# A hybrid decoder step on one core: matmul order pinned by hand, or left to the scheduler under the same priorities

## The chip, the core and the metric

The kernel runs on one core of a Trainium2 chip. The core has TensorE (matmul, PE in the profile), VectorE (DVE), ScalarE (ACT), GpSimd (POOL) and the SP queue, which issues all DMAs here. Each engine works through its own list of instructions in order and waits on semaphores where an operand comes from another engine. The metric is the time of one execution on the device in microseconds, the median of the runs.

## The reference, cut to what matters

One inference step of a one-layer decoder for 1024 prompt tokens and 8 x 4 sample tokens, model width 1024. All is in 32-bit floats.

```
h = RMSNorm(x);  z = h @ w_in            # 7944 columns, split among mixers and gates
ya = gated DeltaNet(z_a)                  # 4 heads of 128: conv, SiLU, chunked delta rule
yb = RWKV-7(z_b)                          # 8 heads of 64: shift, LoRA decay, delta state update
yc = RG-LRU(z_c)                          # conv, gates, diagonal scan
x = x + (sum_b sigmoid(z_gate_b) * (y_b @ w_branch[b])) @ w_out
x = x + relu(RMSNorm(x) @ w_up)^2 @ w_down
y = RMSNorm(x)
```

The two delta rules are recurrences over tokens. Both are written in chunks: inside a chunk a triangular matrix of products of keys is inverted, and between chunks a state is handed on, so each chunk's output waits for the state of the one before.

## The kernel before

**Projections.** Every large product is computed as three matmuls of a 128x128 weight with a 128x352 slice of the tokens (high by high, low halves by high), on PSUM tiles named g, whose rotation has two buffers. `weights` loads a weight tile (wraw), ScalarE rounds it to its high half (whi, L342), and VectorE or, in the recurrence, GpSimd subtracts to get the low half (wlo, L343). `gemm_steps` is a generator: one step is three matmuls, and a projection of 128 output channels is 24 steps of 72 matmuls in all. ScalarE copies the result out (z).

**The recurrence.** After the start (norm, the RG-LRU branch, and half of the projections of branches A and B) comes a stage of 18 units. A unit is one segment of 128 tokens (one of every nine is the 32 sample tokens) of two RWKV head pairs (`rwkv_seg`) and two DeltaNet heads (`gdn_seg`), with one joint inversion of their triangular blocks. The steps of a unit that the change and the trace speak of:

- Gram matmuls: rr<-AR,BK (L1092), masked by VectorE into GM (L1095). AR and BK are products that VectorE and GpSimd form (L1070 to L1083); the two halves of the first BK product run on GpSimd, those of the second on VectorE (L1080 to L1082).
- `inv16_load`: GM and LA are written to DRAM and read back as rows of 16x16 blocks, i16m (L842 to L846).
- `inv16_solve`: some 24 VectorE operations on 48 rows invert these blocks (L858 to L886); the result i16z goes to DRAM and comes back as i16u (L894, L897).
- `tri`: it is spread (ixt, L903), transposed (ix, L924) and completed to 64x64 and 128x128 inverses (inv, TT) in alternating matmuls (rr<-ix,GM and others) and copies.
- The links: sr<-N,AR (with the old state N), tm (L1181), sr<-tm,inv, UV (L1185, L1186), sr<-UV,BT and sr<-UV,GM, then the new N (L1217, L1218). There are two links to a unit. DeltaNet's one link is sg<-St,kq, gtm, sg<-gtm,TT, gu, sg<-gu,kv, St.
- Reciprocal square roots, `rsqrt` (L641 to L652): an integer guess and three Newton steps on 128x2 or 128x4 numbers, 13 operations on GpSimd, three times a unit: tile nwyg for the keys' norm, nwyo and nwyr for the two output norms.

**What sets the order.** A scheduler builds each engine's list. It takes the ready instruction of highest priority, by its own estimate of when operands are ready; priority is program order unless `high_priority` raises it, and `keep_in_program_order` fixes an instruction in the list where the program has it. Program order comes from `PLAN` (L1474), a table of 19 places: at each, some steps of the new unit ("n..") or of the old one ("o..") are issued, and then `fill.go(2)` issues two steps (six matmuls) of the projections still to do: in units 0 to 8 the other half of branches A and B, then the merge gates. While the stage runs (`T.on`), `Ordered._pin` fixes every TensorE instruction at its place, the old unit's steps and the inversion get high priority on the other engines, and projections that are left when the units are done follow in `fill.rest()`. All TensorE work passes through `Ordered`, so the profile of the kernel before gives one line for all matmuls (L259) and one for all transposes (L262); they are told apart by tile names.

**Behind the stage** come the merge of the branches, the output projection and the feed-forward part, nearly all projections.

Of the kernel before, what the change touches and what calls it, by code (L numbers as in the profile page):

```python
# [10 lines left out]
I32 = mybir.dt.int32  # L11
# [237 lines left out]
class Ordered:  # L249


    def __init__(self, tc, eng):
        self.tc, self.eng, self.on = tc, eng, False

    def _pin(self, r):
        return self.tc.keep_in_program_order(r) if self.on else r

    def matmul(self, *a, **kw):
        return self._pin(self.eng.matmul(*a, **kw))  # L259

    def transpose(self, *a, **kw):
        return self._pin(self.eng.transpose(*a, **kw))  # L262


# [30 lines left out]
class K:  # L295
    def __init__(self, tc, ctx, ap):
        self.tc, self.nc, self.ap = tc, tc.nc, ap
        self.ctx = ctx
        self.V, self.A, self.P, self.T, self.S = (tc.nc.vector, tc.nc.scalar, tc.nc.gpsimd, Ordered(tc, tc.nc.tensor), tc.nc.sync)
        self.n = 0  # L300
        self.lo_eng = tc.nc.vector
# [127 lines left out]
def build(tc, ap):  # L429
    nc = tc.nc  # L430
    with ExitStack() as ctx:
# [209 lines left out]
        def rsqrt(x, shape, tag):  # L641

            yi = k.tile(mp, shape, "nwy" + tag, 2, I32)
            t = k.tile(mp, shape, "nwt" + tag, 1)
            P.tensor_scalar(out=yi, in0=x.bitcast(I32), scalar1=-0.5, scalar2=1597463007.0, op0=ALU.mult, op1=ALU.add)
            y = yi.bitcast(F32)
            for _ in range(3):
                P.tensor_tensor(out=t, in0=y, in1=y, op=ALU.mult)
                P.tensor_tensor(out=t, in0=t, in1=x, op=ALU.mult)
                P.tensor_scalar(out=t, in0=t, scalar1=-0.5, scalar2=1.5, op0=ALU.mult, op1=ALU.add)  # L650
                P.tensor_tensor(out=y, in0=t, in1=y, op=ALU.mult)
            return y  # L652
# [328 lines left out]
        def prio():  # L981

            return nullcontext() if T.on else tc.high_priority()
# [16 lines left out]
        def rwkv_seg(R, seg, J):  # L1000

            s2, lora = R["s2"], R["lora"]
            if True:
# [76 lines left out]
                for src, j, e in ((kk, 0, P), (zk, 1, V)):  # L1080
# [380 lines left out]
        T.on = True  # L1461
# [16 lines left out]
        for i in range(19):  # L1478
            after_ = None
            for what, f in PLAN:  # L1480
                for w_ in what.split():
# [5 lines left out]
                    elif w_ in ("load", "solve"):  # L1487
                        if new:
                            with tc.high_priority():
                                (inv16_load if w_ == "load" else inv16_solve)(new["J"])  # L1490
                    else:
                        u = new if w_[0] == "n" else old
                        if u:
                            with tc.high_priority() if w_[0] == "o" else nullcontext():
                                next(u[w_[1]], None)
# [5 lines left out]
        T.on = False  # L1501
# [183 lines left out]
```

## Time and profile before

| | |
|---|---|
| median of 3 runs | 2503.41 us (2502.68 to 2505.58) |
| the profiled execution | 2511.07 us, its span 2509.3 us |
| TensorE busy | 2183.4 us, 87% of the span |
| VectorE, ScalarE, GpSimd busy | 1178.8, 816.8, 512.2 us |
| mean granted TensorE clock | 0.925 |
| the stage of 18 units | about 380 to 1430 us |

The page's second part cuts the span into 40 slices of 62.7 us, each digit the busy share in tenths. A wait view says which engine stood still for whose result; a timeline shows each instruction with its start, its duration and, in brackets, the idle time of its engine before it and what ended that. A matmul of the small kind stands as two records in the trace, so counts there are twice those of the program's order. Busy times of a matmul overlap its neighbours'; the distance between two starts is what one costs.

### The profile page before, as it was taken

To read this page: it belongs to the slowest core of one execution; us is meant where nothing else is said; L and a number is where in the kernel's file an instruction comes from. 1 tells how busy PE (TensorE), PEld (TensorE's weight loads), DVE (VectorE), ACT (ScalarE), POOL (GpSimd) and SP (SyncE) were. 2 spreads that over 40 slices of the span, in tenths; PEclk is the share of its full clock that TensorE was granted. 3 is DMA by queue.
4 is the path that set the end of the run, shared out by engine and by line. 5 is a ranking of instruction groups with operands and counts; after the bars stand their busy time and mean duration, and the time that the engine had idled before them with its cause. 6 is when DMAs were issued, how large, how long until landed. Compare 5 with 4: busy or idle time off the path is not lost. (4 is left out here: it accounts for less than half of the span.)

```text
span 2509.3 us, 42716 instructions
## 1 busy us (share of the span) xinstructions
PE 2183.4 (87%) x16939; PEld 2042.7 (81%) x16939; DVE 1178.8 (47%) x2490; ACT 816.8 (33%) x1915; POOL 512.2 (20%) x1213
## 2 busy tenths in 40 slices
PE   8999987776667677777777899999999999999997
PEld 7998986666556565666656799999999999999997
DVE  7453353555555544455445205747433433333336
ACT  5564342333333332243333222225221221221224
POOL 2013233333324223233343220013000000000003
PEclk9999996888887887888888899999999999999999
DMA  4114331222222222222221335433111111111114
GB/s 132 67 57 135 101 100 57 77 66 55 56 60 69 62 66 77 57 68 64 62 55 50 106 129 193 151 120 109 43 46 48 47 47 43 51 43 47 47 44 148
DMA packets 171713, 191.59 MB, mean 76 GB/s; under 512 B 60853, under 2 KB 114293, under 8 KB 171513
## 3 DMA queue, kind: packets, MB, share of 16 engines
q1 hardware_dynamic: 171512, 188.87, 24.6%
q8 instruction: 133, 2.18, 0.4%
q14 instruction: 68, 0.55, 0.1%
HBM read 140.68 MB, written 48.13 MB: 75 GB/s over the span
## 5 line engine op out<-in xcount | busy, mean ns | idle before, releaser
L259 PE MATMUL g<-hhi,whi 128*128 128x352 f32 x2664 | 904.5, 346 | 15.3 <-DVE z L419 14.0
L259 PE MATMUL g<-hhi,wlo 128*128 128x352 f32 x2568 | 848.5, 330 | 0.9 <-POOL wlo L343 0.9
L259 PE MATMUL g<-hlo,whi 128*128 128x352 f32 x2472 | 819.3, 331 | 4.6 <-DVE hlo L561 3.4
L259 PEld LDWEIGHTS g<-hhi,whi 128*128 128x128 f32 x2664 | 516.4, 195 | 34.6 <-DVE z L419 16.1
L259 PEld LDWEIGHTS g<-hhi,wlo 128*128 128x128 f32 x2568 | 501.1, 195 | 2.2 <-POOL wlo L343 1.4
L259 PEld LDWEIGHTS g<-hlo,whi 128*128 128x128 f32 x2472 | 485.4, 196 | 9.3 <-DVE hlo L561 4.5
L342 ACT CAST whi<-wraw 128x512 fp32r<-128x512 f32 x326 | 200.9, 619 | 558.2 <-PE g L259 545.8
L259 PE MATMUL g<-ahi,wlo 128*128 128x352 f32 x768 | 248.4, 323 | 0.0
L259 PE MATMUL g<-ahi,whi 128*128 128x352 f32 x768 | 248.3, 323 | 0.0
L259 PE MATMUL g<-alo,whi 128*128 128x352 f32 x768 | 248.1, 323 | 0.0
L1586 POOL TENSOR_TENSOR acc<-acc,sq 128x352 f32<-128x352 f32 x36 | 37.2, 1033 | 913.3 <-ACT sq L1585 912.7
L343 DVE TENSOR_TENSOR wlo<-wraw,whi 128x512 fp32r<-128x512 f32 x216 | 151.6, 703 | 146.8 <-ACT whi L342 142.8
L343 POOL TENSOR_TENSOR wlo<-wraw,whi 128x512 fp32r<-128x512 f32 x110 | 147.4, 1343 | 338.9 <-ACT whi L342 322.6
L1647 DVE TENSOR_TENSOR x<-g,x 128x352 f32<-128x352 f32 x192 | 100.4, 524 | 201.1 <-PE g L259 201.1
L259 PE MATMUL rr<-ix,GM 32*32 32x32 f32 x816 | 19.0, 224 | 171.0 <-DVE ix L924 171.0
L259 PEld LDWEIGHTS rr<-ix,GM 32*32 32x32 f32 x816 | 14.7, 134 | 178.2 <-DVE ix L924 129.3
L259 PEld LDWEIGHTS g<-ahi,wlo 128*128 128x128 f32 x768 | 144.8, 189 | 0.1
L259 PEld LDWEIGHTS g<-ahi,whi 128*128 128x128 f32 x768 | 144.6, 188 | 0.2
L259 PEld LDWEIGHTS g<-alo,whi 128*128 128x128 f32 x768 | 144.6, 188 | 0.1
L1636 DVE TENSOR_TENSOR rl<-rl,g 128x352 f32<-128x352 f32 x96 | 49.8, 519 | 133.5 <-ACT rl L1635 133.5
L1635 ACT ACTIVATE rl<-g 128x352 f32<-128x352 f32 x96 | 44.4, 463 | 138.5 <-PE g L259 138.5
L1638 DVE TENSOR_TENSOR alo<-rl,ahi 128x352 fp32r<-128x352 f32 x96 | 50.4, 525 | 47.5 <-ACT ahi L1637 47.5
(354 smaller groups left out, 2920.6 us busy)
## 6 DMA issues: line engine op xcount, KB each, us to landing
wraw<-win SPq DMA_DIRECT2D x126, 256.0 KB, 2.7
wraw<-wdn SPq DMA_DIRECT2D x80, 256.0 KB, 2.6
wraw<-wup SPq DMA_DIRECT2D x64, 256.0 KB, 2.6
scr_t<-z SPq DMA_DIRECT2D x24, 528.0 KB, 3.2
tgl<-scr_t SPq DMA_DIRECT2D x24, 528.0 KB, 4.1
scr_za<-z SPq DMA_DIRECT2D x16, 528.0 KB, 3.0
wraw<-wout SPq DMA_DIRECT2D x32, 256.0 KB, 2.6
scr_zb<-z SPq DMA_DIRECT2D x12, 528.0 KB, 2.7
```

Source lines behind the costliest of these rows:

```text
L259: return self._pin(self.eng.matmul(*a, **kw))
L342: self.A.copy(hi, r3)
L343: self.lo_eng.tensor_tensor(out=lo, in0=r3, in1=hi.bitcast(F32), op=ALU.subtract)
L1586: (V if last else P).tensor_tensor(out=acc[g], in0=acc[g], in1=sq, op=ALU.add)
L1635: A.activation(out=rl, in_=ps, func=AF.Relu)
L1636: V.tensor_tensor(out=rl, in0=rl, in1=ps, op=ALU.mult)
L1638: V.tensor_tensor(out=b[:, gl(g)], in0=rl, in1=a[:, gl(g)].bitcast(F32), op=ALU.subtract)
L1647: V.tensor_tensor(out=x2[c][:, gl(g)], in0=ps, in1=x2[c][:, gl(g)], op=ALU.add)
```

## The change

TensorE's instructions are no longer pinned: `Ordered` is gone, and a flag `k.busy` takes over its other use (it keeps the extra priority of some elementwise steps off during the stage). The raised priority of the old unit's steps and of the inversion is gone too, so within the stage program order alone is the priority on all engines, apart from the weights' halves and the copies out of PSUM. `rsqrt` moves from GpSimd to VectorE, with two operations of a Newton step merged: 10 operations instead of 13. The first BK product moves from GpSimd to VectorE.

```diff
--- before.py
+++ after.py
@@ -246,22 +246,6 @@
 
 
 
-class Ordered:
-
-
-    def __init__(self, tc, eng):
-        self.tc, self.eng, self.on = tc, eng, False
-
-    def _pin(self, r):
-        return self.tc.keep_in_program_order(r) if self.on else r
-
-    def matmul(self, *a, **kw):
-        return self._pin(self.eng.matmul(*a, **kw))
-
-    def transpose(self, *a, **kw):
-        return self._pin(self.eng.transpose(*a, **kw))
-
-
 def run(gen):
 
     while True:
@@ -296,8 +280,9 @@
     def __init__(self, tc, ctx, ap):
         self.tc, self.nc, self.ap = tc, tc.nc, ap
         self.ctx = ctx
-        self.V, self.A, self.P, self.T, self.S = (tc.nc.vector, tc.nc.scalar, tc.nc.gpsimd, Ordered(tc, tc.nc.tensor), tc.nc.sync)
+        self.V, self.A, self.P, self.T, self.S = (tc.nc.vector, tc.nc.scalar, tc.nc.gpsimd, tc.nc.tensor, tc.nc.sync)
         self.n = 0
+        self.busy = False
         self.lo_eng = tc.nc.vector
 
     def pool(self, name, bufs=1, side=None, psum=False):
@@ -642,13 +627,12 @@
 
             yi = k.tile(mp, shape, "nwy" + tag, 2, I32)
             t = k.tile(mp, shape, "nwt" + tag, 1)
-            P.tensor_scalar(out=yi, in0=x.bitcast(I32), scalar1=-0.5, scalar2=1597463007.0, op0=ALU.mult, op1=ALU.add)
+            V.tensor_scalar(out=yi, in0=x.bitcast(I32), scalar1=-0.5, scalar2=1597463007.0, op0=ALU.mult, op1=ALU.add)
             y = yi.bitcast(F32)
             for _ in range(3):
-                P.tensor_tensor(out=t, in0=y, in1=y, op=ALU.mult)
-                P.tensor_tensor(out=t, in0=t, in1=x, op=ALU.mult)
-                P.tensor_scalar(out=t, in0=t, scalar1=-0.5, scalar2=1.5, op0=ALU.mult, op1=ALU.add)
-                P.tensor_tensor(out=y, in0=t, in1=y, op=ALU.mult)
+                V.tensor_tensor(out=t, in0=y, in1=y, op=ALU.mult)
+                V.scalar_tensor_tensor(out=t, in0=t, scalar=-0.5, in1=x, op0=ALU.mult, op1=ALU.mult)
+                V.scalar_tensor_tensor(out=y, in0=t, scalar=1.5, in1=y, op0=ALU.add, op1=ALU.mult)
             return y
 
         def store_tail(dst, z, sv, hist):
@@ -980,7 +964,7 @@
 
         def prio():
 
-            return nullcontext() if T.on else tc.high_priority()
+            return nullcontext() if k.busy else tc.high_priority()
 
         def rwkv_gemm(s2):
             lo = k.tile(mp, [128, 2, 3, 128], "lora", 1)
@@ -1077,7 +1061,7 @@
                 for i in range(2):
                     A.activation(out=pr(av, i), in_=pr(av, i), func=AF.Identity, scale=k.p("bka", 2 * s2 + i), bias=k.d("oka", 2 * s2 + i))
                 V.tensor_tensor(out=ch(zk), in0=ch(zk), in1=ch(av), op=ALU.mult)
-                for src, j, e in ((kk, 0, P), (zk, 1, V)):
+                for src, j, e in ((kk, 0, V), (zk, 1, V)):
                     for h in range(2):
                         e.tensor_tensor(out=BK[H[h], 0:nb, j if h == 0 else 1 - j, 0:tl], in0=ch(src)[H[h]], in1=ch(ei)[H[h]], op=ALU.mult)
                 V.tensor_tensor(out=ar(1), in0=ch(zr), in1=ch(eg), op=ALU.mult)
@@ -1458,7 +1442,7 @@
             return r, g
 
         rb, ra = run(rwkv_gemm(0)), run(gdn_gemm(0))
-        T.on = True
+        k.busy = True
         fill = Filler(second_half())
 
         def unit(i):
@@ -1486,19 +1470,16 @@
                         after_ = unit(i + 1) if i < 17 else None
                     elif w_ in ("load", "solve"):
                         if new:
-                            with tc.high_priority():
-                                (inv16_load if w_ == "load" else inv16_solve)(new["J"])
+                            (inv16_load if w_ == "load" else inv16_solve)(new["J"])
                     else:
                         u = new if w_[0] == "n" else old
                         if u:
-                            with tc.high_priority() if w_[0] == "o" else nullcontext():
-                                next(u[w_[1]], None)
+                            next(u[w_[1]], None)
                 fill.go(f)
             if i == 0:
                 fill.go(14)
             new, old = after_, new
         fill.rest()
-        T.on = False
         mp_cm.__exit__(None, None, None)
 
         mg_cm = k.pool("mrg", side="left")
```

What this does to the order, at three places. Line numbers of the changed kernel are 16 to 19 lower.

First, TensorE between DeltaNet's last step and the Gram matmuls of the next unit, in the unit of masks GM_1715; g tiles are projections. Before:

```order
L259 MATMUL sr_11288<-tm_11289,inv_11074 64x64 x4
L259 MATMUL sg_11273<-gu_11270,kv_10541 128x128 x2
L259 MATMUL sg_11273<-gu_11270,LA_10540 128x128 x2
L259 MATMUL rr_11346<-kq_10854 128x256
L259 MATMUL rr_11352<-kq_10854 128x256
L259 MATMUL g_11303<-hhi,whi_10992 128x352
L259 MATMUL g_11303<-hlo,whi_10992 128x352
L259 MATMUL g_11303<-hhi,wlo_10993 128x352
L259 MATMUL g_11303<-hhi,whi_10992 128x352
L259 MATMUL g_11303<-hlo,whi_10992 128x352
L259 MATMUL g_11303<-hhi,wlo_10993 128x352
L259 MATMUL rr_11365<-AR_11083,BK_11084 128x128
```

The same place in the changed kernel:

```order
L1076 MATMUL rr_11248<-AR_10972,BK_10973 128x128
L1145 MATMUL sr_11108<-UV_10756,BT_10675 64x64 x4
L1145 MATMUL sr_11108<-UV_10756,GM_10662 64x64 x4
L1076 MATMUL rr_11249<-AR_10972,BK_10973 128x128
L1076 MATMUL rr_11248<-AR_10972,BK_10973 128x128
L1076 MATMUL rr_11249<-AR_10972,BK_10973 128x128
L1076 MATMUL rr_11248<-AR_10972,BK_10973 128x128
L1076 MATMUL rr_11249<-AR_10972,BK_10973 128x128
L1076 MATMUL rr_11248<-AR_10972,BK_10973 128x128
L1076 MATMUL rr_11249<-AR_10972,BK_10973 128x128
L1085 MATMUL rr_11261<-con,BK_10973 128x128
L1145 MATMUL sr_11174<-N_11151,AR_10371 64x64 x8
```

Six projections stand no longer between DeltaNet's step and the Gram matmuls; the first link's last matmuls (sr<-UV) stand among them, and the second link (sr<-N,AR) behind them, where it stood ahead.

Second, TensorE behind the output transposes of DeltaNet (rr<-con,oa) in that unit. Before:

```order
L262 MATMUL rr_11549<-con,oa_11268 128x128 x2
L259 MATMUL g_11542<-hhi,whi_11481 128x352
L259 MATMUL g_11542<-hlo,whi_11481 128x352
L259 MATMUL g_11542<-hhi,wlo_11482 128x352
L259 MATMUL g_11542<-hhi,whi_11481 128x352
```

Changed:

```order
L1413 MATMUL rr_11429<-con,oa_11154 128x128
L1145 MATMUL sr_11693<-N_11289,AR_10972 64x64 x3
L1413 MATMUL rr_11429<-con,oa_11154 128x128
L1145 MATMUL sr_11693<-N_11289,AR_10972 64x64 x5
L340 MATMUL g_12063<-hhi,whi_12059 128x352
L341 MATMUL g_12063<-hlo,whi_12059 128x352
```

The first matmuls of the next unit's first link (sr<-N,AR) now stand here, ahead of that unit's inverse. Counted in the order, the projections between the matmuls rr<-con,k (L1242) and the next rr<-ix,GM are 18 before and 64 in the changed kernel.

Third, VectorE from the masks to the solve. Before:

```order
L1095 TENSOR_TENSOR GM_10770<-rr_10771,con 128x512
L1095 TENSOR_TENSOR GM_10770<-rr_10772,con 128x512
L1217 TENSOR_TENSOR N_10812<-sr_10695,N_10656 128x128
L1229 TENSOR_REDUCE mv_10816<-k_1685_10613 128x4
L1218 TENSOR_TENSOR N_10812<-N_10812,wc_9915 128x128
L1230 TENSOR_SCALAR mv_10816<-mv_10816 128x4
L1231 TENSOR_TENSOR k_1685_10613<-k_1685_10613,mv_10816 128x256
L1126 TENSOR_TENSOR zv_10233<-rr_10879,zv_10233 128x256
L1233 TENSOR_REDUCE mv_10816<-k_1723_10815 128x4
L1234 TENSOR_SCALAR mv_10816<-mv_10816 128x4
L1236 TENSOR_TENSOR k_1685_10613<-k_1685_10613,nwyr_10823 128x256
L858 COPY i16z_10906<-i16m_10795 48x8
```

Changed, the rows just ahead of the solve (L842 there is L858 before):

```order
L1321 TENSOR_TENSOR ar_11237<-con,gr_10740 128x128
L1217 TENSOR_REDUCE mv_10708<-k_1723_10707 128x4
L1414 SCALAR_TENSOR_TENSOR zg_9570<-rr_10828,d_hang,zg_9570 128x256
L1218 TENSOR_SCALAR mv_10708<-mv_10708 128x4
L630 TENSOR_SCALAR nwyr_10715<-mv_10708 128x4
L633 TENSOR_TENSOR nwtr_10716<-nwyr_10715 128x4
L634 SCALAR_TENSOR_TENSOR nwtr_10716<-nwtr_10716,mv_10708 128x4
L635 SCALAR_TENSOR_TENSOR nwyr_10715<-nwtr_10716,nwyr_10715 128x4
L633 TENSOR_TENSOR nwtr_10716<-nwyr_10715 128x4
L634 SCALAR_TENSOR_TENSOR nwtr_10716<-nwtr_10716,mv_10708 128x4
L842 COPY i16z_10795<-i16m_10687 48x8
L853 COPY i16z_10795<-i16m_10687 48x4x2x2
```

The root of the RWKV output norm (nwyr) ran on GpSimd between the two rows mv and k; now its steps stand in VectorE's list, some ahead of the solve and some between its first steps, and DeltaNet's output product zg stands ahead of it.

## Rows read from the trace of the kernel before

**Rows 1.** The page, parts 1 and 2: busy times, TensorE's slices, its granted clock.
```profile
PE 2183.4 (87%) x16939; PEld 2042.7 (81%) x16939; DVE 1178.8 (47%) x2490; ACT 816.8 (33%) x1915; POOL 512.2 (20%) x1213
PE   8999987776667677777777899999999999999997
PEclk9999996888887887888888899999999999999999
```

**Rows 2.** The waits: engine, line waited for: total us, times, longest.
```profile
PE rr L259 <- DVE ix L924: 171.0, 18, 12.6
DVE k L1236 <- POOL nwyr L651: 55.9, 17, 3.7
DVE gsl L1320 <- POOL nwyg L651: 27.2, 17, 3.8
```

**Rows 3.** Line L924 alone: durations in ns, first and last start.
```profile
L924 DVE STREAM_TRANSPOSE ix<-ixt x18: 311/378/379, 380.3 to 1388.8; 128x192 f32<-128x192 f32 x16, 128x128 f32<-128x128 f32 x2
```

**Rows 4.** Windows: busy us by engine, granted clock, DMA share, GB/s.
```profile
1061.00:1115.00 54.00, 39.38 (x466) 34.33 (x466) 28.14 (x73) 18.94 (x59) 18.21 (x51) 0.88 0.27 74
1430.00:1525.00 95.00, 94.63 (x596) 94.34 (x595) 13.72 (x17) 26.70 (x46) 16.50 (x12) 1.00 0.48 162
1800.00:1900.00 100.00, 100.00 (x625) 100.00 (x624) 39.41 (x72) 22.69 (x44) 0.00 (x0) 1.00 0.15 48
```

**Rows 5.** Timeline of TensorE, one unit: start us, us, operation, [idle before].
```profile
1006.41 0.65 PE L259 MATMUL rr<-ix,GM 32*32 32x32 f32 x32 [8.34 <-DVE ix L924]
1007.96 0.49 PE L259 MATMUL g<-hhi,wlo 128*128 128x352 f32 x1
1008.25 0.49 PE L259 MATMUL g<-hhi,whi 128*128 128x352 f32 x1
1033.61 1.16 PE L259 MATMUL rr<-AR,BK 64*128 64x128 f32 x16
1051.39 0.32 PE L259 MATMUL g<-hhi,wlo 128*128 128x352 f32 x1
1061.12 0.65 PE L259 MATMUL rr<-ix,GM 32*32 32x32 f32 x32 [9.40 <-DVE ix L924]
```

**Rows 6.** A window behind such a wait.
```profile
1008.00:1010.00 2.00, 2.00 (x53) 1.61 (x52) 0.00 (x0) 0.92 (x2) 0.22 (x1) 0.50 0.03 8
```

**Rows 7.** Timeline of VectorE, the same unit.
```profile
1023.44 1.61 DVE L1082 TENSOR_TENSOR BK<-zk,k 64x256 f32<-64x256 f32 x2
1034.80 1.29 DVE L1095 TENSOR_TENSOR GM<-rr,con 128x512 f32<-128x512 f32 x2 [0.63 <-PE rr L259]
1046.33 1.48 DVE L1236 TENSOR_TENSOR k<-k,nwyr 128x256 f32<-128x256 f32 x1 [3.70 <-POOL nwyr L651]
1047.74 0.16 DVE L858 COPY i16z<-i16m 48x8 f32<-48x8 f32 x1
1048.00 0.16 DVE L870 TENSOR_TENSOR i16t<-i16z 48x8 f32<-48x8 f32 x1
1048.20 0.17 DVE L871 TENSOR_TENSOR i16z<-i16z,i16t 48x8 f32<-48x8 f32 x1
1060.29 0.36 DVE L903 TENSOR_TENSOR ixt<-i16u,con 128x192 f32<-128x192 f32 x1 [5.81 <-DMA i16u<-scr_i]
```

**Rows 8.** Timeline of GpSimd, the same unit.
```profile
1042.72 0.19 POOL L645 TENSOR_SCALAR nwyr<-mv 128x4 int32<-128x4 int32 x1 [1.72 <-DVE mv L1234]
1046.25 1.28 POOL L343 TENSOR_TENSOR wlo<-wraw,whi 128x512 fp32r<-128x512 f32 x1
```

**Rows 9.** Timeline of the SP queue, the same unit.
```profile
1039.24 0.33 SPq L846 DMA_DIRECT2D i16m<-scr_i  x1
```

**Rows 10.** Line L846, read back of the Gram matrix: time to landing.
```profile
DMA to landing us min/median/max: 1.9/2.5/3.5
```

**Rows 11.** Lines L1082 and L1236 alone: ns min/median/max.
```profile
L1082 DVE TENSOR_TENSOR BK<-zk,k x36: 216/422/2040, 355.1 to 1352.0; 64x256 f32<-64x256 f32 x32, 64x64 f32<-64x64 f32 x4
...
L1236 DVE TENSOR_TENSOR k<-k,nwyr x18: 281/426/1489, 448.3 to 1420.4; 128x256 f32<-128x256 f32 x16, 128x128 f32<-128x128 f32 x2
```

## The prediction

> **What bounds the kernel now.** I read the page from the top, then the waits of TensorE, then one unit of the recurrence on the timelines. The reader sees first that TensorE is busy 87% of the span, and that the loss has one place: the slices from about 380 to 1430 us stand at 6 to 8 tenths with a granted clock of 0.8, while the slices of the last third stand at 9 and 9 [rows 1]. In that third 625 matmuls fill 100 us, so a projection matmul of 352 columns costs 0.160 us at the full clock [rows 4]. The staged stretch is therefore where a new order can give or take anything. Its beat is one unit of the recurrence; the inverse's transpose (L924) stands once in each of 18 units, from 380.3 to 1388.8 us, which is 1008.5 / 17 = 59.3 us a unit [rows 3]. A quiet unit is 54 us [rows 4].
>
> Among TensorE's waits one rules: 171.0 us in 18 waits for that same transpose [rows 2], 9.5 us a unit. The timeline of a unit shows why [rows 5, 7 to 9]. The unit's Gram matmuls (AR, BK) start at 1033.61, the masks at 1034.80, the matrix is read back from DRAM at 1039.24, the 16x16 solve starts at 1047.74, its result is back at 1060.29, and TensorE, idle since 1051.7, starts on it at 1061.12. So a unit has two parts. Part A runs from one inverse to the next masks, 1006.41 to 1034.80, 28.4 us; part B from the masks to the inverse, 1034.80 to 1061.12, 26.3 us, and for its last 9.4 us TensorE has nothing. After such a wait the granted clock is 0.50, that is 1.2 GHz [rows 6], and the projection matmuls come 0.29 us apart [rows 5].
>
> **The change part by part.** *Tail.* Counted in the order of the two programs, the matmuls on g tiles behind the last unit's second product of its inverse (rr<-ix,GM, L943) are 6684 before and 6448 after: 236 projections are drawn into the staged stretch. They leave a stretch in which TensorE is busy 94.63 of 95 us [rows 4], so they give 236 x 0.160 = 37.8 us there. Inside, their cover is the idle time before the inverse: 13 matmuls a unit, 2.1 us of 9.5. If that cover is gone they cost the same 37.8 us and this term is 0.
>
> *Part A.* From inverse to Gram matmuls the old order has 54 projections and about 135 small matmuls, in nearly every unit (96 in the first); the new one 23 to 43 projections, mostly about 33 (50 in the first), and about 100 small ones. What left is the old unit's second link, and the first link of the next, which now stands before the inverse. That is 21 projections less, 21 x 0.160 = 3.4 us (6.1 us if all ran at 0.29), and some 35 small ones, which I estimate at 2 us (the eight Gram matmuls, two records each and the dearest kind, take 1.16 us [rows 5], 0.145 each; the links' are 64x64 and I count 0.04 to 0.07, which gives 1.4 to 2.5). TensorE's part is thus 4.8 to 8.6 us shorter; I take 5.4. What is late next is VectorE: its last BK product ends at 1025.05 [rows 7], 18.6 us behind the inverse, so A cannot fall under some 20 us while TensorE was the later of the two by 8.6. Into this part VectorE takes over the ten-step root of the keys and the beta product. A dependent small operation follows another by 0.20 us [rows 7], so ten cost 2.0 us; the two beta halves cost 0.42 us each at the median of the same product there [rows 11]. Against that stand VectorE's waits for GpSimd's root, 27.2 us in 17 = 1.6 a unit [rows 2]. Sum: +2.8 - 1.6 = +1.2, which I round up to +1.4. Part A: -5.4 + 1.4 = -4.0 us. Its bounds are 0 and -7.2 (8.6 less 1.4).
>
> *Part B.* The read back is issued 4.4 us behind the masks [rows 7, 9] and lands 2.5 us later [rows 10], at 1041.7. VectorE takes the solve up only at 1047.74: it stands at L1236 for GpSimd's root, from 1042.72 on, 55.9 us in 17 waits = 3.3 us a unit over the kernel [rows 2, 7, 8]. That wait goes. What is late next is VectorE itself: between masks and solve it now has some 28 rows, the whole output root and half of the other among them. At 0.20 us for the small half and 0.3 to 0.45 for the rest that is about 8.5 us, so the solve starts 8.5 us behind the masks and no longer 12.9: -4.4. The rest of the root steps and zg then lie between the solve's own, about eight more at 0.20 = +1.4 (where an operation stands, it is not free). Another +1.5 I allow for the hops of that root through ScalarE to TensorE and back, on which zg now waits in front of the solve. Sum -1.5 us, with -4.4 and +4 (all twenty root steps at 0.20 in the way and nothing gained) as bounds. Behind TensorE's Gram matmuls the new order has 81 to 113 projections instead of 60, so 92 x 0.160 + 80 x 0.055 = 19 us of work; it still reaches the inverse early, and the wait shrinks from 9.5 to about 5 us. That this wait is covered is not a gain of its own: the loop over DRAM sets part B.
>
> *GpSimd and SP.* GpSimd loses 39 root steps and two products a unit; it was on no bound. SP's order keeps the solve's store behind the y stores and one z store, as before, and nothing on it is dearer.
>
> At one place a rule can be weighed. GpSimd's low-half subtraction starts at 1046.25 and takes 1.28 us; VectorE's product with the root starts at 1046.33 and takes 1.48 us [rows 7, 8], where the median of that line's 18 is 0.43 [rows 11]. The Trainium skill, SBUF — State Buffer, section "SBUF: two separate sides", says that the two engines share a port pair under an exclusive lock, and that a VectorE operation with two SBUF inputs waits out a GpSimd one in full. By that rule nearly all root steps can be held so, but 41 fewer GpSimd instructions a unit stand against them; that the trace agrees is seen in these two rows.
>
> **The sum.** Per unit -4.0 - 1.5 = -5.5 us, 18 times -99.0, tail -37.8: -136.8 us. The profiled execution took 2511.07 us (its span of 2509.3 and 1.8 around it), which gives 2374.3; the runs' median, 2503.41, lies 7.7 under that execution, so 2366.6, and I say 2366 us. A difference under 0.2% (5 us) can't be told from no change.
>
> **The rivals.** *The chain links lose their cover, and it is slower.* In the old order six projections, about 1 us, stand behind every link of the recurrence; in the new one the second link's matmuls stand among small ones alone, and TensorE waits for each answer in order, with what is queued behind. For it: TensorE runs in order, and a wait brings the clock to 0.50 [rows 6]. Against it: the old wait of 9.5 us is far larger than these. Eight links uncovered by 1.1 us each are +8.8, less the 4.0 of part A = +4.8 us a unit: 2503.4 + 18 x 4.8 - 37.8 = 2552 us. It decides from the point at which part A of a quiet unit is longer than today's 28.4 us. Chance 0.15.
>
> *The loop over DRAM and VectorE keeps its beat.* What TensorE saves in part A it then waits before the masks; only the tail is left: 2503.4 - 37.8 = 2466 us. For it: VectorE is busy 28.1 of 54 us [rows 4] and gets about 5 more. Against: TensorE was 8.6 us behind VectorE at the Gram matmuls. Chance 0.12.
>
> *VectorE and GpSimd collide.* As in the pair of rows above, each low-half subtraction that meets a root step holds it 1.1 us; three meetings a unit beyond today's are +3.3 us, 18 times 59: 2366 + 59 = 2425 us. Against it: GpSimd is busy 18 of 54 us today and about half of that after. Chance 0.13. This is also what the rule named above would make of the change if GpSimd's remaining work met it.
>
> *It does more.* If A falls to the 21 us that VectorE needs and B by its bound of 4.4, a unit loses 7.2 + 4.4 = 11.6 us: 2503.4 - 208.8 - 37.8 = 2257 us. A middle of this and the forecast, 2310, is likelier than the end. Chance 0.13 for all below 2320.
>
> That the change spreads the projections is not what the order shows: it gathers 64 of them before the inverse and thins them between the links. The argument above does not need them spread.
>
> **How the numbers follow.** The forecast has 0.47, its own range is 2320 to 2430. Low is 2285, between the forecast and the full gain, which leaves about 0.08 below; high is 2500, past the case of the tail alone, and leaves the most of the slower rival, about 0.12. Faster by over 0.2%: the forecast, the collisions, the tail alone and the larger gain, 0.85 less some 0.05 for their far ends, 0.80. Slower 0.15, and 0.05 for within 0.2%.
>
> **What would show it.** The transposes of the inverse 53 to 54 us apart on the mean; TensorE's wait for them near 5 us a unit; Gram matmuls about 24 us behind the inverse in a quiet unit; the solve starting about 8.5 us behind the masks, with no wait for GpSimd's roots; a granted clock over 0.9 in the staged stretch; the bare stretch before the merge shorter by 38 us. I am wrong if new waits of TensorE on sr and sg tiles add up to more than the wait on ix gives back, or if part B grows because the roots stand in the solve's way.

## The result and the profile after

The changed kernel takes 2224.81 us (median of 4, 2220.14 to 2227.51) against 2504.29 (2502.68 to 2505.58): a ratio of 0.888, interval 0.886 to 0.890. It is 280 us faster; 138 had been forecast, and the range ended at 2285. The direction was right, the size was not. Where executions of one kernel differ, ratios leave out those more than 1.5% above its fastest.

First the page of the changed kernel, parts 1 and 2, as in [rows 1].

```profile
PE 2137.2 (96%) x16939; PEld 2003.5 (90%) x16939; DVE 1236.4 (56%) x3066; ACT 817.3 (37%) x1915; POOL 349.8 (16%) x475
PE   8998999999999999999999999999999999999997
PEclk9999999999999999999999999999999999999998
```

The dip of 6 to 8 tenths is gone: TensorE has the same 16939 matmul records and is busy in 96% of a span that is 291 us shorter: 245 us less idle time (326 to 81 us) and 46 us less busy time, at a higher clock. The windows show where the time went: first the stage (from the first to the last inverse) and a stretch behind it in the kernel before, then the same two in the changed one (columns as in [rows 4]). The stretch holds the projections that are left and the beginning of the merge; its end lies equally far from the end of both kernels.

```profile
380.00:1389.00 1009.00, 735.75 (x7870) 622.42 (x7870) 510.37 (x1316) 329.42 (x1007) 338.96 (x941) 0.84 0.23 63
1430.00:1590.00 160.00, 159.63 (x1004) 159.34 (x1003) 53.99 (x87) 38.53 (x62) 16.50 (x12) 1.00 0.52 172
```

```profile
376.00:1139.00 763.00, 723.97 (x8086) 615.09 (x8086) 564.72 (x1863) 335.15 (x1019) 192.79 (x248) 0.97 0.31 87
1184.00:1300.00 116.00, 116.00 (x731) 116.00 (x731) 52.99 (x88) 27.65 (x42) 5.90 (x5) 1.00 0.54 179
```

The stage does 216 records more in 246 us less: TensorE's idle time there falls from 273 to 39 us and its granted clock rises from 0.84 to 0.97. The stretch behind has 273 records less and is 44 us shorter; in it TensorE has projections alone up to the merge's first product, at 1510.0 us before and at 1218.2 in the changed kernel. Those two are the 291 us but for a unit's end and the start, which change by 4 us each, in opposite ways.

The beat of the units, to be held against [rows 3], and TensorE's waits for the inverse, against [rows 2], and for UV of a link (27.5 us before, shown further down):

```profile
L908 DVE STREAM_TRANSPOSE ix<-ixt x18: 306/378/381, 376.2 to 1138.8; 128x192 f32<-128x192 f32 x16, 128x128 f32<-128x128 f32 x2
```

```profile
PE rr L912 <- DVE ix L908: 20.1, 15, 3.0
PE sr L1145 <- DVE UV L1170: 5.0, 8, 1.1
```

A unit is now (1138.8 - 376.2) / 17 = 44.9 us, no longer 59.3. From the starts of every unit's transpose and first mask in the timelines, part A is 21.1 us on the mean and was 33.9; part B is 23.8 and was 25.5. One quiet unit of the changed kernel, TensorE, then VectorE (columns as in [rows 5, 7]):

```profile
925.15 0.45 PE L912 MATMUL rr<-ix,GM 32*32 32x32 f32 x32 [0.65 <-DVE ix L908]
927.09 0.71 PE L1019 MATMUL rr<-ll,lora 64*128 64x128 f32 x8
940.20 0.48 PE L1076 MATMUL rr<-AR,BK 64*128 64x128 f32 x2
967.12 0.45 PE L912 MATMUL rr<-ix,GM 32*32 32x32 f32 x32 [0.68 <-DVE ix L908]
```

```profile
938.68 0.87 DVE L1066 TENSOR_TENSOR BK<-zk,k 64x256 f32<-64x256 f32 x2
943.95 0.68 DVE L1079 TENSOR_TENSOR GM<-rr,con 128x512 f32<-128x512 f32 x1
953.38 0.17 DVE L842 COPY i16z<-i16m 48x8 f32<-48x8 f32 x1 [0.57 <-DMA i16m<-scr_i]
953.65 0.16 DVE L854 TENSOR_TENSOR i16t<-i16z 48x8 f32<-48x8 f32 x1
953.74 0.15 DVE L634 SCALAR_TENSOR_TENSOR nwtr<-nwtr,mv 128x4 f32<-128x4 f32 x1
953.85 0.17 DVE L855 TENSOR_TENSOR i16z<-i16z,i16t 48x8 f32<-48x8 f32 x1
```

The Gram matmuls start 15.0 us behind the inverse (27.2 in [rows 5]), the last BK product ends 14.4 us behind it (18.6 in [rows 7]). In this unit the solve no longer waits for a root but for its own read back. TensorE, which stood 9.4 us before the inverse, stands 0.7.

### The profile page after: what moved, and what is told of

Read it like the earlier page. It is cut to its first block, busy times and chain, and to the rows that moved or that the text cites. A ratio compares the mean times of both kernels' runs of the same rounds, so it can differ in the third digit from the quotient of the medians.

```text
span 2218.4 us, 42560 instructions
## 1 busy us (share of the span) xinstructions
PE 2137.2 (96%) x16939; PEld 2003.5 (90%) x16939; DVE 1236.4 (56%) x3066; ACT 817.3 (37%) x1915; POOL 349.8 (16%) x475
## 3 DMA queue, kind: packets, MB, share of 16 engines
q1 hardware_dynamic: 171512, 188.87, 27.5%
## 4 chain that ended last, share of the span: by engine, by line
PE 74%; DVE 14%; DMA 4%; ACT 2%; issue 2%; POOL 1%; SPq 1%; DVEq 0%; POOLq 0%; ACTq 0%
PE g L341 21%; PE g L340 21%; PE g L342 21%; DVE i16p L864 2%; PE sr L1145 2%; DMA i16u<-scr_i 1%; DMA scr_i<-i16z 1%; DVE BK L1066 1%; DMA i16m<-scr_i 1%; PE rr L1076 1%; PE rr L775 1%; PE rr L1019 1%; DVE hf L515 1%; DVE i16z L870 1%; PE sg L1351 1%
## 5 line engine op out<-in xcount | busy, mean ns | idle before, releaser
L340 PE MATMUL g<-hhi,whi 128*128 128x352 f32 x2568 | 849.6, 331 | 15.1 <-DVE z L404 12.5
L341 PE MATMUL g<-hlo,whi 128*128 128x352 f32 x2472 | 811.4, 328 | 3.4 <-DVE hlo L546 2.1
L340 PEld LDWEIGHTS g<-hhi,whi 128*128 128x128 f32 x2568 | 488.1, 190 | 26.3 <-DVE z L404 15.2
L342 PEld LDWEIGHTS g<-hhi,wlo 128*128 128x128 f32 x2568 | 488.2, 190 | 7.3 <-POOL wlo L328 2.3
L341 PEld LDWEIGHTS g<-hlo,whi 128*128 128x128 f32 x2472 | 471.0, 191 | 11.0 <-DVE hlo L546 3.4
L1618 ACT CAST ahi<-rl 128x352 fp32r<-128x352 f32 x96 | 46.7, 487 | 63.2 <-DVE rl L1617 63.2
L1429 ACT ACTIVATE z<-g 128x352 f32<-128x352 f32 x72 | 33.2, 461 | 84.4 <-PE g L342 83.4
```

The source lines that it names most:

```text
L340: T.matmul(ps, whi(k), xhi(k), start=start and k == ks[0], stop=False)
L341: T.matmul(ps, whi(k), xlo(k), start=False, stop=False)
L342: T.matmul(ps, wlo(k), xhi(k), start=False, stop=stop and k == ks[-1])
L1618: A.copy(a[:, gl(g)], rl)
```

## The experiments

All ratios are to the kernel before on the same chip, with 95% intervals. "Released" is a kernel in which TensorE is not fixed in program order.

**Three edits, alone and in pairs.** The title speaks of the same priorities, but the change drops the raised ones and moves work between engines as well. It has three parts: TensorE released, priorities dropped, roots and first beta product (the first BK product) on VectorE. The edits are

```diff
-        return self.tc.keep_in_program_order(r) if self.on else r
+        return r
```

```diff
-                            with tc.high_priority():
-                                (inv16_load if w_ == "load" else inv16_solve)(new["J"])
+                            (inv16_load if w_ == "load" else inv16_solve)(new["J"])
...
-                            with tc.high_priority() if w_[0] == "o" else nullcontext():
-                                next(u[w_[1]], None)
+                            next(u[w_[1]], None)
```

and, for the third, the hunks of `rsqrt` and of the BK loop as they stand in the change. Expected of each alone, and of the first two together:

Released alone: 

> The kernel before with TensorE's instructions no longer fixed at their place; raised priorities and GpSimd's roots and beta product stay. Theory 1 (the fixed order of TensorE held the recurrence back: in every unit the next unit's first links and 54 projections stood ahead of the Gram matmuls): most of the 280 us goes with this edit alone, so 2230 to 2330 us, the unit 45 to 50 us, part A (inverse to masks) about 22 us on the mean. Theory 2 (VectorE's waits for GpSimd's roots set the beat, 83 us in all): little, 2440 to 2510 us. Theory 3 (raised priorities put the old unit's work ahead on VectorE and ScalarE): little, above 2440 us.

Priorities dropped alone: 

> The kernel before without the raised priorities of the old unit's steps and of the inversion; TensorE stays fixed in order, roots and beta product stay on GpSimd. Theory 1: TensorE's list is unchanged word for word, so within 1%, 2480 to 2525 us. Theory 2: no change or slightly slower, since the solve stands later on VectorE. Theory 3: 2300 to 2420 us.

Roots and beta product moved alone: 

> The kernel before with the roots and the first beta product on VectorE; TensorE stays fixed in order, raised priorities stay. Theory 1: the solve starts earlier, but part A stays at 30 us or more: a gain of 1 to 4 us a unit, 2430 to 2490 us. Theory 2: VectorE's waits of 83 us go and part B shortens with them, 2340 to 2430 us. Theory 3: 2460 to 2510 us.

Released, priorities dropped: 

> The kernel before with TensorE not fixed and without raised priorities; roots and beta product stay on GpSimd, so that only this part of the change is missing. Theory 1: close to the changed kernel, 2225 to 2290 us, with VectorE's waits for GpSimd's roots still there but covered, since TensorE has 79 to 107 projections behind the Gram matmuls. Theory 2: above 2350 us. Theory 3: as theory 1.

Released, roots moved: 

> The changed kernel with the raised priorities of the old unit's steps and of the inversion put back: TensorE not fixed, roots and beta product on VectorE. Theory A (two separate causes, TensorE's fixed order and the roots on GpSimd; the dropped priority gives nothing): the two ratios multiply, 0.929 x 0.960 = 0.892, so 2215 to 2250 us. Theory B (TensorE is now the bound, so what else shortens the loop no longer counts): the same as the changed kernel within 0.6%, 2210 to 2238 us. Theory C (dropping the priority is what brings the two together): 2270 us or more, near the mean of the kernels with one edit.

Fixed, priorities dropped, roots moved: 

> The changed kernel with TensorE fixed in the order of before; roots and beta product on VectorE, no raised priority. Theory A: the pin costs its 7% here too: 2400 to 2440 us (2407 x 1.010 = 2431). Theory C: the dropped priority helps once the roots are on VectorE: 2300 to 2390 us. A rival that the roots were the main thing all along: below 2330 us.

Part A and part B are means over the units, in us.

| kernel | us | ratio | part A | part B |
|---|---|---|---|---|
| before | 2508 | 1 | 33.9 | 25.5 |
| released | 2328 | 0.929 (0.926 to 0.932) | 23.0 | 26.7 |
| roots moved | 2407 | 0.960 (0.958 to 0.962) | 31.5 | 22.2 |
| priorities dropped | 2534 | 1.010 (1.008 to 1.012) | 35.4 | 25.1 |
| released, dropped | 2356 | 0.940 (0.935 to 0.945) | 24.3 | 27.3 |
| dropped, roots moved | 2457 | 0.980 (0.977 to 0.982) | 34.7 | 22.1 |
| released, roots moved | 2283 | 0.911 (0.907 to 0.915) | 23.8 | 27.2 |
| all three (the change) | 2225 | 0.888 (0.886 to 0.890) | 21.1 | 23.8 |

The release is the larger cause and acts on part A. The roots are the second. Moved alone they take 2.4 us off part A and 3.2 off part B, and the 83 us that VectorE waited for GpSimd [rows 2] go: the 27.2 for the keys' root lay in part A, some 50 of the 55.9 for the output root in part B. In released kernels the two parts no longer tell the time. Released with the roots moved is 45 us faster than released alone with no shorter part, because its stage holds 8300 of TensorE's records instead of 7980.

Theories 1 and 2 each hold for a part, and neither for all: without priorities the fixed kernel is slower than theory 1 allowed, and the released one, at 2356, is as slow as theory 2 had it. Theory 3 alone is wrong. Dropping the priorities costs 1 to 2% in three pairs and gives 2.5% in the fourth, so theory A's product (2237) failed for the released kernel with the roots moved: 2283, as theory C had it. The fixed kernel without priorities and with the roots moved took 2457 us, more than any theory gave it; there dropping the priorities costs 2%, against theory C. Of the four pairs, only the one with TensorE released and the roots moved gains by dropping them.

**The place of the Gram matmuls, TensorE still fixed.** Is it the free filling by the scheduler, or the place in the list? The table alone was rewritten, so that the Gram matmuls come ahead of the second link:

```diff
-        PLAN = (("nr ot", 2), ("ng ot", 2), ("ot or", 2), ("ot or", 2), ("or og", 2), ("or og", 2), ("or og ng", 2), ("nr load", 2),
-                ("or unit", 2), ("nr", 2), ("nr", 2), ("solve", 2), ("og", 2), ("", 2), ("or", 2), ("", 2), ("", 2), ("nt", 2),
+        PLAN = (("nr ot", 2), ("ng ot", 2), ("ot or ng", 2), ("ot nr load", 2), ("or og", 2), ("or og", 2), ("or og", 2), ("or", 2),
+                ("or unit", 2), ("nr", 2), ("nr", 2), ("solve", 2), ("og", 2), ("", 2), ("or", 2), ("", 2), ("", 2), ("nt", 2),
```

Rewritten table alone: 

> The kernel before, TensorE fixed, priorities raised and roots on GpSimd as before; only the table is rewritten: the new unit's Gram matmuls stand four places earlier, with 30 projections instead of 54 between inverse and Gram matmuls and 84 instead of 60 behind them, and the old unit's second link and DeltaNet's last steps behind them. Theory J (it is the place of the Gram matmuls in TensorE's list that counts, whoever writes it): part A falls from 34 to 22 to 25 us and the unit to 48 to 52 us, 2330 to 2400 us, close to the kernel with TensorE released alone (2328). Theory K (it is the free filling of TensorE's waits by the scheduler that counts): 2450 us or more.

With the roots moved too: 

> The same rewritten table with TensorE fixed and priorities raised, and the roots and the first beta product on VectorE besides. Theory J: both causes together as in the changed kernel, 2215 to 2300 us. Theory K: not below 2360 us (2407 with the old table).

Measured: 2426 us, 0.967 (0.965 to 0.968), and 2342 us, 0.933 (0.932 to 0.935). The table gives 82 us and then 65 on top of the roots, about half of what the release gives, and both times lie between the two theories. Part A falls to 22.4 and 19.8 us, as far as theory J asked, but part B grows from 25.5 to 32.1 and from 22.2 to 30.1: what was moved behind the Gram matmuls is now in VectorE's way there. In the first of the two kernels the solve takes 12.7 us on the mean instead of 8.7, and from its end to the transpose pass 9.9 instead of 6.2. The waits of TensorE in the same kernel:

```profile
PE rr L259 <- DVE BK L1082: 72.1, 16, 6.1
PE rr L259 <- ACT UV L1118: 37.0, 11, 4.8
PE rr L259 <- DVE ix L924: 17.2, 9, 2.7
```

A fixed list waits at the Gram matmuls, 4.5 us a time, for BK, and nothing behind them can go ahead. The wait for the inverse falls from 171 us to 17, but the new waits take back a good part of it. The rest of the gain came only with the released list; which of its moves bring it is not shown.

**Is TensorE the bound now?** One more copy through DRAM in every second unit's inversion lengthens the loop over DRAM; three steps of projections at a place of the table draw more into the stage; and the rewritten table, put into the changed kernel, shortens part A.

```diff
+            if J["i"] % 2:
+                dr2 = tc.dram_tile([2, nt, 64, 16], F32, name=f"scr_j{k.n}")
+                S.dma_start(dr2, dr)
+                dr = dr2
             u = k.tile(mp, [128, 6, 16], "i16u", 2)[:, :nt]
...
-            J = {}
+            J = {"i": i}
```

```diff
-                fill.go(f)
+                fill.go(f if i < 9 else 3)
```

Copy, kernel before: 

> The kernel before with the same copy through DRAM in the same 9 units. TensorE's list is unchanged and has nothing left behind the 60 projections, so the hop is not covered: 9 times 3 to 5 us, 2530 to 2550 us. If the loop over DRAM does not set the beat of before: within 0.3%, 2500 to 2512 us.

Copy, changed kernel: 

> The changed kernel with one more copy through DRAM in the inversion of every second unit (9 of 18), between the solve's store and its read back, so that the loop over DRAM gets longer there by the hop and nothing else. Theory B (TensorE is the bound and the scheduler fills the longer wait with projections from the bare stretch): the stage gets longer, the bare stretch shorter by the same, the whole time within 0.6% of the changed kernel, 2210 to 2240 us. Theory D (the loop over DRAM still sets the beat): 9 times the hop of 3 to 5 us on top, 2252 to 2270 us.

More projections: 

> The changed kernel with three steps of projections at each place of the table in units 9 to 17 instead of two; 277 projections more are then drawn from the bare stretch into the stage, 44 us. Theory B (TensorE is the bound; what is moved from one place to the other is paid in both): the bare stretch 40 to 45 us shorter, the stage longer by the same, 2210 to 2240 us. Theory I (the stage has idle time left for them): 2180 to 2205 us. If they push the recurrence behind them: 2250 us or more.

Rewritten table: 

> The changed kernel with the rewritten table (Gram matmuls ahead of the second link) in program order, so in priority. Theory B (TensorE is full in the stage, so a shorter loop finds no room): within 0.6%, 2210 to 2238 us. If the loop still sets the beat: part A under 19.5 us and 2160 to 2200 us.

And raised priority for the inversion besides: 

> As the run before, with raised priority for the inversion's load and solve besides. Theory B: 2205 to 2235 us, no different from the changed kernel. If the loop sets the beat: below 2190 us.

The copy costs the kernel before 20 us (2529.5 against 2509.8, ratio 1.009, 1.006 to 1.011), 2.2 us a time, at the lower edge of what was expected: its loop over DRAM did set the beat. The changed kernel with the copy takes 2266 us, 41 more than without, and with more projections 2246, 21 more. The first lies in theory D's range, but 9 times 2.2 us are 20, not 41, and the trace shows another mechanism; the second lies above theory B's range. The waits of TensorE in these two, in that order:

```profile
PE rr L916 <- DVE ix L912: 25.5, 11, 12.5
PE g L340 <- ACT yhi L1504: 15.2, 4, 11.0
```

```profile
PE rr L912 <- DVE ix L908: 28.7, 16, 4.5
PE g L340 <- ACT yhi L1500: 15.7, 4, 10.2
```

In both the projections have run out at the end: the merge's longest wait for the last unit's outputs (yhi) is 11.0 and 10.2 us, and with the copy TensorE has nothing to do for 12.5 us before the last unit's inverse. In the changed kernel the merge does not wait for yhi; the projections left behind its stage, 34 us of the 116, are no loss but the cover of the last unit.

In the stage itself the longer loop is covered: with the copy it is 71 us longer, for 410 records more (66 us at 0.160 each), and TensorE's idle time there is 51 us instead of 39, the difference being the last unit's 12.5. There the loop over DRAM no longer sets the beat. With three steps the stage is 811.4 us long, 48.8 more, for 245 records more; these are 39 us at 0.160, so the exchange is not quite even.

The rewritten table in the changed kernel answers it too: 2221.8 us, 0.886 (0.884 to 0.888), and 2223.5, 0.887 (0.885 to 0.890), no difference from the change. Part A is 16.7 us in the first of them, 4.3 less, part B 27.9, 4.1 more, the unit 44.6. A shorter part A brings nothing, with TensorE busy in 96% of the span. That part B grew by as much could by itself be the moved work. But with the inversion raised besides the stage is 745.7 us long, 17 less than in the change, and the time is the same: what the stage no longer holds is done behind it.

The page and the wait for the inverse in the first:

```profile
PE 2133.9 (96%) x16939; PEld 1999.3 (90%) x16939; DVE 1225.7 (55%) x3066; ACT 817.5 (37%) x1915; POOL 339.9 (15%) x475
PE rr L912 <- DVE ix L908: 13.3, 15, 1.9
```

**Which priority, which operation.** The changed kernel with raised priority for the inversion alone, for the old unit alone, and with the first beta product back on GpSimd:

```diff
-                            (inv16_load if w_ == "load" else inv16_solve)(new["J"])
+                            with tc.high_priority():
+                                (inv16_load if w_ == "load" else inv16_solve)(new["J"])
```

```diff
-                            next(u[w_[1]], None)
+                            with tc.high_priority() if w_[0] == "o" else nullcontext():
+                                next(u[w_[1]], None)
```

```diff
-                for src, j, e in ((kk, 0, V), (zk, 1, V)):
+                for src, j, e in ((kk, 0, P), (zk, 1, V)):
```

Inversion raised: 

> The changed kernel with raised priority for the inversion's load and solve alone; the old unit's steps stay at program order. Theory G (it is the old unit's raised priority that costs the 58 us between the changed kernel and the one with both priorities, since it leaves 21 instead of 33 projections between inverse and Gram matmuls): 2210 to 2240 us, TensorE's clock in the stage 0.96 or more. Theory H (it is the inversion's priority): 2265 to 2300 us.

Old unit raised: 

> The changed kernel with raised priority for the old unit's steps alone; the inversion stays at program order. Theory G (the old unit's raised priority is what costs the 58 us): 2265 to 2300 us with the masks 10 us ahead of the read back instead of 6 and a granted clock of the whole near 0.955. Otherwise, if only both priorities together cost it: 2215 to 2240 us.

Beta product on GpSimd: 

> The changed kernel with the first beta product back on GpSimd; the roots stay on VectorE. If the roots are what the move to VectorE is worth: 2215 to 2245 us. If the beta product counts as much as the roots: 2270 to 2300 us (half of the 131 us between the changed kernel and the one with both on GpSimd).

Measured: 2222.5 us, 0.887 (0.885 to 0.888); 2286.6 us with four executions spread from 2258 to 2317, and a ratio of 0.903 (0.899 to 0.908) from the two shorter ones; 2237.2 us, 0.893 (0.891 to 0.895). So in the released kernel with the roots moved it is the old unit's raised priority that costs, 33 to 92 us by the execution, where both priorities cost 58; the inversion's costs nothing. Theory G holds, with a wider spread than it gave. The roots carry nearly all of the move to VectorE, the beta product 12 us.

**The clock.** Matmuls added ahead of the inverse's first product keep TensorE at work where it waited: 48 of them in the kernel before, 12 in the released one with roots moved and both priorities.

```diff
-            ps = rps32()
+            raw = rps()
+            for _ in range(48):
+                T.matmul(raw[:, 0:GW], k.hhi[:, 0, 0:128], k.hhi[:, 0, 0:GW], start=True, stop=True)
+            ps = raw[:, :nt * 32].rearrange("p (b c) -> p b c", b=nt)
```

Kernel before: 

> The kernel before with 48 matmuls of 128x352 added on TensorE ahead of each unit's first inverse product; their results are overwritten and used by nothing. They are 7.7 us at the full clock, less than the mean wait of 9.5 us in front of that product, so they delay little and leave TensorE no long gap there. Theory E (the low clock behind that wait, 0.50 for several us a unit, is a part of the loss of its own): the granted clock of the stage rises from 0.84 to 0.95 or more and part A gets 2 to 4 us shorter, 18 times: 2430 to 2475 us. Theory F (part A hangs on the order of the links and on VectorE, not on TensorE's speed): within 0.5%, 2495 to 2520 us, or slower by the dummies where the wait is shorter than they are.

Released, roots moved, both priorities: 

> The kernel with TensorE released, roots on VectorE and both priorities raised, with 12 matmuls of 128x352 added ahead of each unit's first inverse product; their results are overwritten and used by nothing, and they cost 1.9 us a unit, about as much as TensorE waits there. Theory L (the 58 us over the changed kernel are the low clock that follows that wait, 176 us at 0.50 in the stage against 44 us in the changed kernel): the granted clock of the stage rises from 0.90 to 0.96 or more, and 40 to 60 us come back less some 10 for the added matmuls: 2230 to 2255 us. Rival M (the loop is longer, its read back comes later, and the clock is beside the point): 2280 to 2310 us.

The first takes 2491 us, 0.994 (0.992 to 0.996); its stage has a granted clock of 0.90 instead of 0.84 and part A is 32.7 instead of 33.9. The time lies between the ranges of theories E and F, nearer to F's. It won back no main part of the loss; how much the whole of the low clock cost is not measured, since more than half of it stayed and the added matmuls can themselves delay the product.

The second takes 2299 us, in rival M's range and no better than 2283. The 216 added matmuls are 216 x 0.160 = 35 us on a full TensorE. The clock of its stage is 0.94 instead of 0.90, but these are the fastest execution of the one kernel and the slowest of the other; over the whole span and four executions each it is 0.962 to 0.969 instead of 0.954 to 0.966. So the added matmuls did little to the clock, and this run does not settle whether the low clock or the later read back makes the 58 us over the changed kernel.

The granted clock of every execution says more. The part of a span that was not granted, span x (1 - clock), is 89 us on the mean of the four executions with both priorities and 46 us in the changed kernel. An estimate from it, for a TensorE that is busy 96% of both spans, is that some 43 of the 58 us are the low clock. The busy times of the profiled executions, 2200.9 against 2137.2 us for the same records, agree; why the clock is lower is not shown.

## Why the prediction was wrong

- **The step that failed** is the term "Part A: -4.0 us. Its bounds are 0 and -7.2". Measured is -12.8 (33.9 to 21.1), 8.8 us a unit more, some 150 us in all. Two things were wrong in it. First, a quiet unit of 28.4 us stood for the mean of 33.9, although the beat used beside it (59.3) was the mean; that makes 5.5 of the 8.8 us. Part A was 57, 50, 42, 38 and 37 us long in five of the 17 units; they are 26, 24, 25, 23 and 21 in the changed kernel. The longest two hold DeltaNet's step for the sample tokens (sg<-ux,kv), all of it ahead of the masks. The release alone does not end them: with the roots moved too and both priorities raised they are still 40 and 40 us, the whole step ahead. They are 26 and 20 under the rewritten table with TensorE fixed, which puts the step behind the masks, and 26 and 24 in the change, where half of it stands behind.
- Second, the other 3.3 us: -4.0 was worked out from the matmuls that left TensorE's list there, with 1.4 us added for VectorE. The mean came out at the bound of this term, 28.4 - 7.2 = 21.2, so what was wrong here is the place within the bounds. The floor of 20 us, taken from VectorE's last BK product, was no property of VectorE: that product stands behind TensorE's LoRA matmuls (rr<-ll,lora), which start 1.9 us behind the inverse in the changed kernel and 4.9 before (1011.32 in the unit of [rows 5], behind 12 projections). BK then ends 14.4 us behind the inverse. On the mean its end moves from 19.4 to 15.8 us with the release alone and to 14.3 in the change, and stays at 19.6 under the rewritten table with TensorE fixed, where the Gram matmuls wait for it. In the changed kernel with the rewritten table part A fell to 16.7 us.
- **Part B**, forecast -1.5, measured -1.7: right in sum, for partly other reasons. The solve starts 9.8 us behind the masks on the mean, not 8.5, and was at 10.5 on the mean before, not 12.9; the solve itself got shorter by 0.8 us (8.7 to 7.9) instead of longer by 1.4. "Where an operation stands, it is not free" did not hold: the solve's dependent operations follow one another by 0.20 us in the fence above (953.65, 953.85) as in [rows 7], with a root step between them at 953.74, and the solve of the quiet unit takes 6.8 us, as against 6.7. The roots' waits were rightly named: moved alone, they give -3.2.
- **Tail**, forecast -37.8, measured -44: near, 273 records instead of 236. But its account as a gain of its own hides what the runs showed: a full TensorE pays for a projection wherever it stands, and most of the gain is the idle time of the stage, 273 to 39 us.
- **The rivals.** The uncovered links did not come: the waits on the links (UV) fell from 27.5 us, the figure of the kernel before, to 5.0. VectorE and GpSimd do not collide more: the product with the root (L1220) has a median of 0.41 us and a longest of 1.49, as in [rows 11], and of the 540 root steps now on VectorE (median 0.16 us) 15 take more than 0.5 us, the longest 1.83. "It does more" was the case that came, and even its end, 2257, was too high, since it too started from the quiet unit; the 4.4 us that it took off part B did not come.

```profile
PE sr L259 <- DVE UV L1186: 27.5, 16, 4.8
```

```profile
L1220 DVE TENSOR_TENSOR k<-k,nwyr x18: 291/413/1485, 418.4 to 1161.1; 128x256 f32<-128x256 f32 x16, 128x128 f32<-128x128 f32 x2
```

- The expected signs held but for size: the clock of the stage is over 0.9, the wait for the inverse is 1.1 us a unit rather than 5, the transposes are 44.9 us apart rather than 53 to 54.

## What to carry to other kernels

A saving per unit has to be taken over all units or from their mean; a quiet one says what the loop could do, not what it costs. An end time on a second engine is a floor only if that engine was not itself waiting for the first: follow its inputs back before using it as a bound. When a fixed list leaves an engine idle in a quarter of a stage, ask first what the time would be with that engine full (idle time and low clock gone), and whether enough independent work is left to fill it to the last unit.

## What was not expected of the hardware

Behind almost the same wait TensorE's clock stays at 0.50 (1.2 GHz) for very different times: some 17 us and some 3 us. In the released kernel with roots moved and both priorities a wait of 1.7 us ends at 1007.0; in the changed kernel one of 2.0 us ends at 1051.3. The windows ahead of it, in the low stretch and behind it, of the first and of the second:

```profile
1003.00:1008.00 5.00, 3.26 (x66) 2.96 (x65) 1.08 (x3) 0.00 (x0) 1.64 (x3) 1.00 0.70 217
1010.00:1022.00 12.00, 12.00 (x89) 9.22 (x87) 5.84 (x12) 6.88 (x24) 0.81 (x2) 0.50 0.09 23
1026.00:1032.00 6.00, 6.00 (x47) 4.72 (x47) 4.15 (x13) 1.30 (x6) 0.00 (x0) 1.00 0.01 3
```

```profile
1046.00:1051.00 5.00, 3.30 (x21) 3.01 (x19) 0.32 (x2) 0.76 (x2) 0.44 (x2) 1.00 0.28 69
1053.00:1056.00 3.00, 3.00 (x23) 2.37 (x23) 1.40 (x3) 1.90 (x6) 1.69 (x2) 0.50 0.25 70
1058.00:1064.00 6.00, 6.00 (x56) 4.88 (x57) 5.71 (x17) 5.64 (x22) 1.70 (x2) 1.00 0.36 125
```

In both TensorE is busy throughout the low stretch, in the first with small matmuls and single projections, in the second with the same small matmuls. Over the stage, windows of 2 us with a clock under 0.75 add up to some 175 us there and to some 45 us in the changed kernel. What brings the clock back sooner is open.

The kernel with the old unit's priority raised spreads over 2258, 2276, 2297 and 2317 us between executions of one program. Their granted clocks are 0.975, 0.968, 0.956 and 0.947, so 56, 73, 101 and 123 us of their spans were not granted. Without these the four agree within 9 us: by this estimate the spread is the clock's.
